# The dt branch of a hybrid block: all 128 partitions, small pieces, a later place in the fill

## The chip, the cores and the metric

The kernel runs on one core of one Trainium2 chip. The metric is device time in microseconds (us) from the first to the last instruction and what lies around them, the median of several runs.

## What is computed

One encoder layer on 512 tokens of width 1024, all in fp32. Cut to what matters here:

```python
h = rms_norm(x, norm1_w)
q, k, v, z, xbc, dt_raw, gate_logits = split_columns(h @ w_in, IN_PROJ_SIZES)
attn = diff_attention(q, k, v, ...) @ w_attn_out          # 8 heads, two softmax maps each
dt_f = softplus(dt_raw[..., :32] + dt_bias_f)              # 32 heads forward, 32 backward
dt_b = softplus(dt_raw[..., 32:] + dt_bias_b)
a_f, a_b = -exp(a_log_f), -exp(a_log_b)
# per chunk of 128 tokens: acs = cumsum(dt * a); exp(acs), exp(acs_last - acs), exp(acs_last) are used
ssd = bi_ssd(...) @ w_ssm_out
x = x + (sigmoid(gate_a) * attn + sigmoid(gate_s) * ssd) @ w_out
x = x + conv_glu(rms_norm(x, norm2_w), ...)
```

The change touches only how the 64 columns of dt_raw are turned into dt and the running sums acs, and when.

## The kernel before

TensorE multiplies in a split form: each fp32 operand is split into hi (rounded, `A.copy` on ScalarE) and lo (`V.tensor_tensor`, the rest, on VectorE), and `mm3` (L201 to L203) makes three matmuls for each 128 rows of the contraction. Weights come through `load_raw` (L133, on SyncE's queue, three buffers `raw`), then as a `RowChunk` (256 columns, two halves of 4 contraction tiles, casts L149 and L150) or a `ColChunk` (two parts of 128 columns, casts L169 and L170), with three buffers each for `whi` and `wlo`.

The first stage is the norm and attention. `attend(fill)` is a planner written out in Python: it keeps a model clock, emits attention's stages (prep: transposes L497; qk: logits L526 and softmax L539 to L546; tr: transposes of the probabilities L552; av: times v L561, with its readers L563 on VectorE and L565 on ScalarE; end: L574 to L580) when their lags are over, and otherwise takes the next step of `fill`. TensorE's instructions run in exactly the order in which this program emits them; the other engines' orders are made by a scheduler. The fill is a chain: the rest of `project(0)`, then `project(1)`, `project(2)`, `project(3)`, then `gate_attn()`. One `project(hp)` makes q, k and v of a pair of heads: three chunks by four token blocks by eight steps of 0.32 us on the model clock, 96 steps, with an evacuation after each block. `v<-mm` (L487) are the four last evacuations of a project; by them project(1) ends near 127 us, project(2) near 181 us and project(3) near 237 us.

PSUM in this stage has eight banks: two under the tag mm (the projections), four under lg (logits), two under t, which everything else shares: tq, ta and av all mean t.

`dt_part` is a generator. It loads 256 columns from C_DT on (only the first 64 are dt), multiplies (`feat_steps`, 8 steps of three matmuls with 512 columns), and works on [64 partitions, 512 tokens]: softplus by a series (L405 to L419: reciprocal in four parts L410, five steps of the series L416), times a (L423), two cumulative sums over 32 partitions each (L426, L427), exp (L428), four stores to DRAM for the later stage (L431). Then eight transposes of 64x128 blocks (L436) into two banks of t, copied out as dtk and acs (L437). Last, selector matmuls (L448) that spread each chunk's last sum, and a tail of two exponentials, a logarithm with its own activation table, and four VectorE operations (L450 to L457). `yield None` ends a piece.

`dt_mixed(fill, dt, lag)` passes the fill's steps on and, each time that they add up to `lag`, takes one piece of dt. Before, the fill given to it is `project(1)`, the lag is 15 us and dt has three pieces: up to the stores; the transposes; the selector and the tail.

Of the kernel before, what the change touches and what calls it, by code (L numbers as in the profile page):

```python
# [8 lines left out]
F32 = mybir.dt.float32  # L9
F32R = mybir.dt.float32r  # L10
# [6 lines left out]
P = 128  # L17
T = 512
D = 1024
NT = T // P  # L20
KD = D // P
# [7 lines left out]
CW = 256  # L29
# [18 lines left out]
def hybrid_block_kernel(ctx: ExitStack, tc, x, w_in, w_attn, w_ssm, w_out, w_up, w_down,  # L48
# [74 lines left out]
    def wtile(tag, shape, dt, bufs):  # L123
        t = wpool.tile([P, 4 * CW], dt, tag=tag, bufs=bufs, name=nm(tag))
        n = shape[0] * shape[1]
        return t[:, :n].rearrange("p (k c) -> p k c", c=shape[1])
# [10 lines left out]
    class RowChunk:  # L137


        def __init__(self, srcs, nk=KD, cw=CW, share=(), between=None):  # L140
            hk = 4 * CW // cw
            self.hk, self.parts = hk, []
            for k0 in range(0, nk, hk):
                n = min(hk, nk - k0)
                raw = load_raw(srcs, k0, n)
                if between and not k0:
                    between()
                hi, lo = wtile("whi", (n, cw), F32R, 3), wtile("wlo", (n, cw), F32R, 3)
                A.copy(hi, raw)  # L149
                (G if k0 in share else V).tensor_tensor(lo, raw, f(hi), SUB)  # L150
                self.parts.append((hi, lo))
# [7 lines left out]
    class ColChunk:  # L159


        def __init__(self, srcs, nk=KD):
            raws = [(k0, min(4, nk - k0), load_raw(srcs, k0, min(4, nk - k0))) for k0 in range(0, nk, 4)]
            self.parts = []
            for j in range(2):
                hi, lo = wtile("whi", (nk, P), F32R, 3), wtile("wlo", (nk, P), F32R, 3)
                for k0, n, raw in raws:
                    src = raw[:, :, j * P:(j + 1) * P]
                    A.copy(hi[:, k0:k0 + n, :], src)  # L169
                    V.tensor_tensor(lo[:, k0:k0 + n, :], src, f(hi[:, k0:k0 + n, :]), SUB)  # L170
                self.parts.append((hi, lo))
# [13 lines left out]
    def wcols(v, c0, n=CW):  # L185
        return v[:, :, c0:c0 + n]
# [99 lines left out]
    def chain(*gens):  # L286
        for g in gens:
            yield from g


    def wide(tag="yb"):
        return mk_yb(tag).rearrange("p a t -> p (a t)")
# [50 lines left out]
    eps = cpool.tile([P, 1], F32, name="eps")  # L343
    elast = cpool.tile([P, NT, 64], F32, name="elast")
    wst = cpool.tile([P, NT, 64], F32, name="wst")
    hd = cpool.tile([64, 2], F32, name="hd")
    na = cpool.tile([64, 1], F32, name="na")

    def table(sp):

# [13 lines left out]
    def parameters(sp):  # L364
        SY.dma_start(pp, pp_d)
        SY.dma_start(rows, rows_d.to_broadcast([P, 4 * 64 + 32]))
        SY.dma_start(hd, hd_d)
        for i in range(2):
            G.tensor_copy(dskip[i * 64:(i + 1) * 64, :], rows[i * 64:(i + 1) * 64, 256 + i::2])
        G.memset(ones, 1.0)  # L370
        G.memset(eps, EPS)
        pr = sp.tile([P, 2, 64], F32, name="pr")
        lv = rows[:, 0:256].rearrange("p (a b d) -> p a b d", a=2, b=2)
        G.tensor_tensor(pr, lv[:, :, 0, :], lv[:, :, 1, :], MUL)
        ls = sp.tile([P, 2], F32, name="ls")
        V.tensor_reduce(ls, pr, AX.X, ADD)
        A.activation(ls, ls, AF.Exp)
        V.tensor_tensor(nlam, ls[:, 1:2], ls[:, 0:1], SUB)
        V.tensor_scalar(nlam, nlam, -LAMBDA_INIT, None, ADD)

        G.tensor_scalar(pp[:, O_CW:O_SN], pp[:, O_CW:O_SN], 0.5, None, MUL)
        for w in range(3):
            c = O_FW + w * 2 * NF
            G.tensor_scalar(pp[:, c:c + NF], pp[:, c:c + NF], 0.5, None, MUL)
        G.tensor_scalar(pp[:, O_FB:O_FB + NF], pp[:, O_FB:O_FB + NF], 0.5, None, MUL)
        G.tensor_scalar(pp[:, O_QN:O_QN + 1], pp[:, O_QN:O_QN + 1], -0.125, None, MUL)
        G.tensor_scalar(pp[:, O_SUB:O_SUB + 1], pp[:, O_SUB:O_SUB + 1], 1.0 - LAMBDA_INIT, None, MUL)
# [8 lines left out]

    def dt_part(ap):

        wdt = ColChunk([wcols(w_in_v, C_DT, CW)])
        ps = yield from feat_steps(wdt, 0, hT)  # L400

        big = [wide("yo") for _ in range(3)]
        halves = [b[:, i:i + T] for b in big for i in (0, T)]
        xx, u, t, t2, p_ = (h[:64] for h in halves[:5])
        V.tensor_scalar(xx, ps[:64, :], hd[:, 0:1], None, ADD)  # L405
        A.activation(u, xx, AF.Abs)
        A.activation(u, u, AF.Exp, scale=-1.0)
        V.tensor_scalar(t, u, 2.0, None, ADD)
        for c in range(NT):
            V.reciprocal(t2[:, c * P:(c + 1) * P], t[:, c * P:(c + 1) * P])  # L410

        V.tensor_tensor(t, u, t2, MUL)
        A.activation(t2, t, AF.Square)
        A.activation(p_, t2, AF.Copy, scale=1.0 / 13.0)
        for c in (11, 9, 7, 5, 3):
            V.scalar_tensor_tensor(p_, p_, 1.0 / c, t2, ADD, MUL)  # L416
        V.scalar_tensor_tensor(p_, p_, 1.0, t, ADD, MUL)
        V.tensor_scalar(xx, xx, 0.0, None, MAX)
        V.scalar_tensor_tensor(p_, p_, 2.0, xx, MUL, ADD)  # L419
        A.activation(na, hd[:, 1:2], AF.Exp)  # L420
        V.tensor_scalar(na, na, -1.0, None, MUL)
        dtf, da, one, acf = p_, u, t, t2
        V.tensor_scalar(da, dtf, na, None, MUL)  # L423
        G.memset(one, 1.0)
        G.memset(one[:, 0:T:P], 0.0)
        V.tensor_tensor_scan(acf[0:32], one[0:32], da[0:32], 0.0, MUL, ADD)  # L426
        V.tensor_tensor_scan(acf[32:64, ::-1], one[32:64], da[32:64, ::-1], 0.0, MUL, ADD)  # L427
        A.activation(xx, acf, AF.Exp)  # L428
        for src, dst in ((acf, acsD), (xx, eacsD)):
            for d in range(2):  # L430
                SY.dma_start(dst.rearrange("g h d l -> d (g h) l")[d], src[d * 32:(d + 1) * 32])  # L431
        yield None
        for src, dst in ((dtf, dtk), (acf, acs)):
            ps = bank("tq")
            for c in range(NT):
                PE.transpose(ps[:, c * 64:(c + 1) * 64], src[:, c * P:(c + 1) * P], ident[:64, :64])  # L436
            V.tensor_copy(dst.rearrange("p c h -> p (c h)"), ps[:, :256])  # L437
        sel = halves[5][:, :2 * P].rearrange("p (d l) -> p d l", d=2)
        G.memset(sel, 1.0)
        for d, row in ((0, P - 1), (1, 0)):  # L440
            G.affine_select(out=sel[:, d, :], in_=sel[:, d, :], pattern=[[0, P]], compare_op=ALU.is_equal,
                            fill=0.0, base=-row, channel_multiplier=1)
        yield None
        ps = bank("tq")
        psv = ps[:, :256].rearrange("p (c h) -> p c h", h=64)
        for d in range(2):
            for c in range(NT):
                PE.matmul(psv[:, c, d * 32:(d + 1) * 32], lhsT=sel[:, d, :], rhs=acs[:, c, d * 32:(d + 1) * 32],  # L448
                          start=True, stop=True)
        A.activation(elast, psv, AF.Exp)  # L450
        V.tensor_tensor(wst, psv, acs, SUB)
        A.activation(wst, wst, AF.Exp)
        V.tensor_tensor(wst, wst, dtk, MUL)

        V.tensor_scalar(dtk, dtk, 1.0e-37, None, MAX)
        A.activation(dtk, dtk, AF.Ln)
        V.tensor_tensor(acs, dtk, acs, SUB)  # L457

    with pool("attn", side="right", reuse_waits="tile") as ap:
# [196 lines left out]
        def dt_mixed(fill, dt, lag):  # L656

            owed = lag
            for step in fill:
                yield step  # L660
                owed += step
                if owed < lag:
                    continue
                owed = 0.0
                for step in dt:
                    if step is None:
                        break
                    yield step
            run(dt)

        def gate_attn():
            for cb in range(4):
                w = ColChunk([wcols(w_in_v, C_GA + cb * CW)])
                gate_a[cb] = mk_yb()
                for j in range(2):
                    ps = yield from feat_steps(w, j, hT)
                    gate_of(gate_a[cb][:, j, :], ps)
                    yield 0.0
# [13 lines left out]
            next(first)  # L692
        parameters(ap)
        with tc.manual_schedule(engines={mybir.EngineType.PE}):
            attend(chain(first, dt_mixed(project(1), dt_part(ap), 15.0), project(2), project(3), gate_attn()))

    phase["stack"].close()
    open_banks("psum2", mm=3, lg=3, t=2)
# [396 lines left out]
```

## Time and profile before

| | |
|---|---|
| three runs | 1244.09, 1251.4, 1351.95 us |
| median | 1251.4 us |
| profiled execution, its own time | 1247.42 us |
| its span from first to last instruction | 1245.6 us |
| mean granted TensorE clock | 0.997 |
| attention stage | from about 7 us to about 297 us of the span |

A row of the trace gives an engine's work by source line and tile (`out<-in`). PE is TensorE, PEld its weight load, DVE VectorE, ACT ScalarE, POOL GpSimd, SPq SyncE's queue. Idle time of TensorE stands in brackets with what ended it. A matmul's own duration overlaps the next one's, so the time that counts is from start to start.

### The profile page before, as it was taken

What the parts mean: (1) busy time and instruction counts of PE and PEld (TensorE: products, weight loads), DVE (VectorE), ACT (ScalarE), POOL (GpSimd) and SP (SyncE); (2) the same over time, 40 slices, a digit from 0 to 9 for tenths busy, and PEclk for the clock granted to TensorE, in tenths of its full rate; (3) what the DMA queues carried; (4) which work ended last, traced back from release to release, by engine and by line L of the source; (5) the groups of instructions that cost most, each with busy time, mean ns of one, the idle gap of its engine ahead of it and who ended that gap; (6) DMA issues with size and microseconds to landing.
All of it is one profiled execution on the core that took longest, in us unless ns stands there. A gap on an engine that the chain in (4) does not pass through costs nothing.

```text
span 1245.6 us, 17543 instructions
## 1 busy us (share of the span) xinstructions
PE 1228.8 (99%) x6552; PEld 1027.3 (82%) x6552; DVE 800.1 (64%) x1389; ACT 639.2 (51%) x1322; POOL 229.3 (18%) x300
## 2 busy tenths in 40 slices
PE   9989999999999999999999999999999999999998
PEld 7989899988887787887878778877888888888887
DVE  5594757563736897777687876595576766663222
ACT  6573858574524667757465663443344444442211
POOL 3221011103003442513433241140000000000000
PEclk9999999999999999999999999999999999999999
DMA  6241222126443544544444343462123333323341
GB/s 215 85 123 44 74 69 79 53 68 169 132 130 114 166 136 135 152 116 139 142 129 136 121 150 102 135 197 92 48 88 102 102 102 102 101 91 97 113 122 37
DMA packets 115016, 140.32 MB, mean 113 GB/s; under 512 B 5321, under 2 KB 96713, under 8 KB 114930
## 3 DMA queue, kind: packets, MB, share of 16 engines
q1 hardware_dynamic: 107762, 114.02, 29.9%
q0 software_dynamic: 7168, 25.17, 6.7%
q8 instruction: 52, 0.85, 0.3%
q14 instruction: 34, 0.28, 0.1%
HBM read 134.68 MB, written 4.49 MB: 112 GB/s over the span
## 4 chain that ended last, share of the span: by engine, by line
PE 88%; DVE 6%; ACT 3%; issue 1%; DMA 1%; POOL 0%; DVEq 0%; SPq 0%; ACTq 0%; POOLq 0%
PE mm L201 23%; PE mm L202 23%; PE mm L203 23%; PE t L561 2%; PE lg L862 2%; PE t L816 2%; PE lg L856 2%; PE lg L201 1%; PE lg L203 1%; PE lg L202 1%; ACT lg L542 1%; DVE lg L539 1%; DMA raw<-in_w_up_dram 1%; PE t L552 1%; PE t L203 1%
## 5 line engine op out<-in xcount | busy, mean ns | idle before, releaser
L170 DVE TENSOR_TENSOR wlo<-raw,whi 128x512 fp32r<-128x512 f32 x268 | 184.3, 717 | 109.0 <-ACT whi L169 105.3
L169 ACT CAST whi<-raw 128x512 fp32r<-128x512 f32 x268 | 155.1, 618 | 169.7 <-PE mm L202 135.4
L201 PE MATMUL mm<-yo,whi 128*128 128x512 f32 (+1 forms) x552 | 214.7, 390 | 0.0
L203 PE MATMUL mm<-yo,wlo 128*128 128x512 f32 (+2 forms) x552 | 213.9, 388 | 0.0
L202 PE MATMUL mm<-yo,whi 128*128 128x512 f32 (+2 forms) x552 | 213.4, 387 | 0.0
L201 PE MATMUL mm<-h,whi 128*128 128x512 f32 x520 | 208.1, 400 | 0.0
L203 PE MATMUL mm<-h,wlo 128*128 128x512 f32 x520 | 206.2, 397 | 0.0
L202 PE MATMUL mm<-h,whi 128*128 128x512 f32 x520 | 205.4, 395 | 0.0
L201 PEld LDWEIGHTS mm<-yo,whi 128*128 128x128 f32 x552 | 103.4, 188 | 22.5 <-issue 1.2
L202 PEld LDWEIGHTS mm<-yo,whi 128*128 128x128 f32 x552 | 103.6, 188 | 21.3 <-issue 0.7
L203 PEld LDWEIGHTS mm<-yo,wlo 128*128 128x128 f32 x552 | 103.6, 188 | 21.2 <-DVE E L795 0.2
L203 PEld LDWEIGHTS mm<-h,wlo 128*128 128x128 f32 x520 | 97.7, 188 | 22.1 <-issue 2.2
L201 PEld LDWEIGHTS mm<-h,whi 128*128 128x128 f32 x520 | 97.8, 188 | 21.4 <-issue 2.4
L202 PEld LDWEIGHTS mm<-h,whi 128*128 128x128 f32 x520 | 97.8, 188 | 20.8 <-issue 2.0
L201 PE MATMUL mm<-whi,h 128*128 128x256 f32 x384 | 114.9, 300 | 0.0
L150 DVE TENSOR_TENSOR wlo<-raw,whi 128x1024 fp32r<-128x1024 f32 x45 | 55.1, 1225 | 89.2 <-ACT whi L149 89.2
L203 PE MATMUL mm<-whi,h 128*128 128x256 f32 x384 | 110.4, 288 | 0.0
L202 PE MATMUL mm<-wlo,h 128*128 128x256 f32 x384 | 110.1, 287 | 0.0
L794 ACT ACTIVATE E<-E,acs 128x128 f32<-128x128 f32 x256 | 79.0, 390 | 29.7 <-POOL E L790 29.7
L149 ACT CAST whi<-raw 128x1024 fp32r<-128x1024 f32 x46 | 48.4, 1051 | 86.5 <-PE lg L203 39.4
L201 PEld LDWEIGHTS mm<-whi,h 128*128 128x128 f32 x384 | 75.0, 196 | 1.4 <-issue 1.1
L202 PEld LDWEIGHTS mm<-wlo,h 128*128 128x128 f32 x384 | 75.2, 196 | 0.0
(236 smaller groups left out, 2139.1 us busy)
## 6 DMA issues: line engine op xcount, KB each, us to landing
raw<-in_w_in_dram SPq DMA_DIRECT2D x74, 512.0 KB, 4.2
raw<-in_w_up_dram SPq DMA_DIRECT2D x44, 512.0 KB, 4.4
E<-acsD POOLq DMA_DIRECT2D x32, 512.0 KB, 5.2
raw<-in_w_down_dram SPq DMA_DIRECT2D x22, 512.0 KB, 3.8
raw<-in_w_in_dram SPq DMA_DIRECT2D x32, 256.0 KB, 4.4
X<-eacsD POOLq DMA_DIRECT2D x32, 256.0 KB, 4.2
raw<-in_w_ssm_dram SPq DMA_DIRECT2D x16, 512.0 KB, 4.6
yb<-in_x_dram SPq DMA_DIRECT2D x8, 512.0 KB, 6.0
```

Of the source, the lines that this page charges most:

```text
L149: A.copy(hi, raw)
L150: (G if k0 in share else V).tensor_tensor(lo, raw, f(hi), SUB)
L169: A.copy(hi[:, k0:k0 + n, :], src)
L170: V.tensor_tensor(lo[:, k0:k0 + n, :], src, f(hi[:, k0:k0 + n, :]), SUB)
L201: PE.matmul(ps, lhsT=lhi, rhs=rhi, start=first, stop=False)
L202: PE.matmul(ps, lhsT=lhi, rhs=rlo, start=False, stop=False)
L203: PE.matmul(ps, lhsT=llo, rhs=rhi, start=False, stop=last)
L561: PE.matmul(po, lhsT=at[:, kb * P:(kb + 1) * P], rhs=vt[:, kb, hh * P:(hh + 1) * P], start=(kb == 0), stop=(kb == NT - 1))
L794: A.activation(v[:, c, :], v[:, c, :], AF.Exp, bias=acs[:, c, s:s + 1])
L816: PE.matmul(ps[:, :n], lhsT=btok[:, c, :], rhs=xw.rearrange("p d q -> p (d q)")[:, :n], start=True, stop=True)
L856: PE.matmul(py[q:q + 64, l], lhsT=xtok[:, c, j * P + q:j * P + q + 64], rhs=W[:, l], start=True, stop=True)
L862: PE.matmul(ps[:, l], lhsT=S[:, i, j * P:(j + 1) * P], rhs=CT[:, l], start=True, stop=True)
```

## The change

dt moves from the fill of project(1) into that of project(2) and project(3), with a lag of 3.0 us and 22 ends of pieces in place of two. Its 64 weight columns are loaded twice, side by side, so that the product stands on all 128 partitions; the first 64 take tokens 0 to 255, the others tokens 256 to 511, and each elementwise operation covers [128, 256] in place of [64, 512]. The reciprocal is two parts of 128 columns in place of four, the sums are four scans over 32 partitions and 256 columns in place of two over 512, the stores eight in place of four, the transposes four of 128x128 in place of eight. Transposes and selector take their banks from mm in place of t. Two `yo` tiles are held in place of three. `ColChunk` gets a width, so that only one part of 128 columns is cast, where before a second one, which nobody used, was cast too.

```diff
@@ ColChunk
-        def __init__(self, srcs, nk=KD):
+        def __init__(self, srcs, nk=KD, cols=CW):
+            n_ = min(P, cols)
-            for j in range(2):
-                hi, lo = wtile("whi", (nk, P), F32R, 3), wtile("wlo", (nk, P), F32R, 3)
+            for j in range(cols // n_):
+                hi, lo = wtile("whi", (nk, n_), F32R, 3), wtile("wlo", (nk, n_), F32R, 3)
...
@@ parameters
-        SY.dma_start(hd, hd_d)
+        for i in range(2):
+            SY.dma_start(hd[i * 64:(i + 1) * 64], hd_d)
@@ dt_part
-        wdt = ColChunk([wcols(w_in_v, C_DT, CW)])
+        wdt = ColChunk([wcols(w_in_v, C_DT, 64)] * 2, cols=P)
         ps = yield from feat_steps(wdt, 0, hT)
-        big = [wide("yo") for _ in range(3)]
-        halves = [b[:, i:i + T] for b in big for i in (0, T)]
-        xx, u, t, t2, p_ = (h[:64] for h in halves[:5])
-        V.tensor_scalar(xx, ps[:64, :], hd[:, 0:1], None, ADD)
+        big = [wide("yo") for _ in range(2)]
+        xx, u, t, t2, p_, sel = (big[i // 4][:, i % 4 * CW:(i % 4 + 1) * CW] for i in range(6))
+        for i in range(2):
+            r = slice(i * 64, (i + 1) * 64)
+            V.tensor_scalar(xx[r], ps[r, i * CW:(i + 1) * CW], hd[r, 0:1], None, ADD)
+        yield None
         A.activation(u, xx, AF.Abs)
         A.activation(u, u, AF.Exp, scale=-1.0)
         V.tensor_scalar(t, u, 2.0, None, ADD)
-        for c in range(NT):
+        for c in range(2):
+            yield None
             V.reciprocal(t2[:, c * P:(c + 1) * P], t[:, c * P:(c + 1) * P])
+        yield None
...
         for c in (11, 9, 7, 5, 3):
+            yield None
             V.scalar_tensor_tensor(p_, p_, 1.0 / c, t2, ADD, MUL)
+        yield None
         V.scalar_tensor_tensor(p_, p_, 1.0, t, ADD, MUL)
         V.tensor_scalar(xx, xx, 0.0, None, MAX)
+        yield None
...
-        V.tensor_tensor_scan(acf[0:32], one[0:32], da[0:32], 0.0, MUL, ADD)
-        V.tensor_tensor_scan(acf[32:64, ::-1], one[32:64], da[32:64, ::-1], 0.0, MUL, ADD)
+        for r in (0, 64):
+            f_, b_ = slice(r, r + 32), slice(r + 32, r + 64)
+            yield None
+            V.tensor_tensor_scan(acf[f_], one[f_], da[f_], 0.0, MUL, ADD)
+            yield None
+            V.tensor_tensor_scan(acf[b_, ::-1], one[b_], da[b_, ::-1], 0.0, MUL, ADD)
         A.activation(xx, acf, AF.Exp)
         for src, dst in ((acf, acsD), (xx, eacsD)):
-            for d in range(2):
-                SY.dma_start(dst.rearrange("g h d l -> d (g h) l")[d], src[d * 32:(d + 1) * 32])
-        yield None
+            for r in range(4):
+                hf, d = divmod(r, 2)
+                SY.dma_start(dst.rearrange("g h d l -> d (g h) l")[d][:, hf * CW:(hf + 1) * CW],
+                             src[r * 32:(r + 1) * 32])
+        for _ in range(4):
+            yield None
         for src, dst in ((dtf, dtk), (acf, acs)):
-            ps = bank("tq")
-            for c in range(NT):
-                PE.transpose(ps[:, c * 64:(c + 1) * 64], src[:, c * P:(c + 1) * P], ident[:64, :64])
-            V.tensor_copy(dst.rearrange("p c h -> p (c h)"), ps[:, :256])
+            ps = bank("mm")
+            for c in range(2):
+                PE.transpose(ps[:, c * P:(c + 1) * P], src[:, c * P:(c + 1) * P], ident)
+            V.tensor_copy(dst.rearrange("p (f c) h -> p c f h", c=2),
+                          ps[:, :CW].rearrange("p (c f h) -> p c f h", f=2, h=64))
...
-        yield None
-        ps = bank("tq")
+        for _ in range(3):
+            yield None
+        ps = bank("mm")
...
@@ the call
-            attend(chain(first, dt_mixed(project(1), dt_part(ap), 15.0), project(2), project(3), gate_attn()))
+            attend(chain(first, project(1), dt_mixed(chain(project(2), project(3)), dt_part(ap), 3.0), gate_attn()))
```

## Rows read from the trace of the kernel before

**Rows 1.** The page, busy time: engine, busy us (share of span), instructions.
```profile
PE 1228.8 (99%) x6552; PEld 1027.3 (82%) x6552; DVE 800.1 (64%) x1389; ACT 639.2 (51%) x1322; POOL 229.3 (18%) x300
```

**Rows 2.** Timeline of TensorE: start, us, instruction, [idle before it <- what ended it].
```profile
77.50 0.66 PE L552 MATMUL t<-ident,lg 128*128 128x128 f32 x4 [1.89 <-ACT osq L565]
...
88.28 0.66 PE L552 MATMUL t<-ident,lg 128*128 128x128 f32 x4 [1.45 <-ACT osq L565]
...
96.75 0.58 PE L561 MATMUL t<-v,at 128*128 128x128 f32 x1 [2.14 <-DVE dtk L437]
...
147.45 0.71 PE L552 MATMUL t<-ident,lg 128*128 128x128 f32 x4 [1.95 <-ACT osq L565]
...
205.24 0.44 PE L552 MATMUL t<-ident,lg 128*128 128x128 f32 x2 [0.58 <-ACT osq L565]
```

**Rows 3.** Stretches: length, busy us (count) of each engine, granted clock, DMA.
```profile
96.73:100.14 3.41, 3.39 (x16) 3.39 (x17) 0.92 (x3) 0.37 (x2) 0.00 (x0) 0.50 0.00 0
147.93:151.34 3.41, 3.41 (x18) 3.41 (x17) 2.31 (x5) 2.08 (x7) 2.00 (x1) 0.50 0.46 133
```

**Rows 4.** Stretches: dt's time before, then each project, then gate_attn's begin.
```profile
60.00:90.00 30.00, 26.66 (x212) 23.80 (x211) 29.97 (x68) 23.44 (x57) 3.56 (x4) 1.00 0.36 104
...
127.00:180.00 53.00, 51.05 (x414) 48.74 (x414) 32.54 (x77) 36.78 (x90) 8.33 (x8) 0.97 0.23 68
180.00:237.00 57.00, 56.42 (x469) 53.44 (x468) 38.26 (x91) 39.74 (x99) 11.41 (x9) 1.00 0.22 64
...
237.00:262.00 25.00, 25.00 (x144) 19.61 (x144) 20.67 (x56) 20.43 (x49) 0.00 (x0) 1.00 0.28 85
```

**Rows 5.** Groups of VectorE, 53 to 127 us, by shape: busy us, mean ns.
```profile
L410 DVE RECIPROCAL yb<-yb 64x128 f32<-64x128 f32 x4 | 3.4, 897 | 0.0
L416 DVE SCALAR_TENSOR_TENSOR yb<-yb,yb 64x512 f32<-64x512 f32 x5 | 3.4, 672 | 0.0
...
L427 DVE TENSOR_TENSOR_SCAN yb<-yb,yb 32x512 f32<-32x512 f32 x1 | 1.2, 1214 | 0.0
...
L423 DVE TENSOR_SCALAR yb<-yb,na 64x512 f32<-64x512 f32 x1 | 0.5, 473 | 0.0
```

**Rows 6.** Groups of VectorE, other stretches: the same and half the width on 128 partitions.
```profile
L546 DVE SCALAR_TENSOR_TENSOR lg<-lg,rs,lg 128x512 f32<-128x512 f32 x32 | 23.6, 747 | 4.7 <-ACT lg L545 4.4
...
L451 DVE TENSOR_TENSOR wst<-t,acs 128x256 f32<-128x256 f32 x1 | 0.4, 420 | 0.0
```

**Rows 7.** The page, costliest groups and DMA issues: casts of a ColChunk, weight loads.
```profile
L170 DVE TENSOR_TENSOR wlo<-raw,whi 128x512 fp32r<-128x512 f32 x268 | 184.3, 717 | 109.0 <-ACT whi L169 105.3
...
raw<-in_w_in_dram SPq DMA_DIRECT2D x74, 512.0 KB, 4.2
```

**Rows 8.** Timelines of TensorE and VectorE, 93 to 97 us: transposes, then the copies.
```profile
93.26 0.81 PE L436 MATMUL t<-ident,yb 64*128 64x64 f32 x8
...
95.29 0.75 DVE L546 SCALAR_TENSOR_TENSOR lg<-lg,rs,lg 128x512 f32<-128x512 f32 x1
...
96.28 0.41 DVE L437 COPY dtk<-t 128x256 f32<-128x256 f32 x1
96.62 0.41 DVE L437 COPY acs<-t 128x256 f32<-128x256 f32 x1
```

**Rows 9.** Timeline of VectorE around the end of project(3).
```profile
234.78 0.29 DVE L563 COPY osb<-t 128x128 f32<-128x128 f32 x1 [1.72 <-PE t L561]
236.15 0.75 DVE L504 SCALAR_TENSOR_TENSOR qkl<-t,pp,qkh 128x512 fp32r<-128x512 f32 x1 [1.07 <-ACT qkh L503]
236.82 0.68 DVE L170 TENSOR_TENSOR wlo<-raw,whi 128x512 fp32r<-128x512 f32 x1
```

**Rows 10.** Timeline of ScalarE: dt's tail with the logarithm's table and the exponential's.
```profile
126.74 0.37 ACT L450 ACTIVATE elast<-t 128x256 f32<-128x256 f32 x1
...
130.95 1.28 ACT L456 ACT_TABLE_LOAD   x1
132.45 0.42 ACT L456 ACTIVATE dtk<-dtk 128x256 f32<-128x256 f32 x1 [0.22 <-DVE dtk L455]
132.89 1.28 ACT L542 ACT_TABLE_LOAD   x1
```

More of the change, by code (lines that the diff above doesn't have):

```diff
@@ L159, in hybrid_block_kernel @@
     class ColChunk:
-        def __init__(self, srcs, nk=KD):
+        def __init__(self, srcs, nk=KD, cols=CW):
+            n_ = min(P, cols)
             raws = [(k0, min(4, nk - k0), load_raw(srcs, k0, min(4, nk - k0))) for k0 in range(0, nk, 4)]
             self.parts = []
-            for j in range(2):
-                hi, lo = wtile("whi", (nk, P), F32R, 3), wtile("wlo", (nk, P), F32R, 3)
+            for j in range(cols // n_):
+                hi, lo = wtile("whi", (nk, n_), F32R, 3), wtile("wlo", (nk, n_), F32R, 3)
                 for k0, n, raw in raws:
-                    src = raw[:, :, j * P:(j + 1) * P]
+                    src = raw[:, :, j * n_:(j + 1) * n_]
                     A.copy(hi[:, k0:k0 + n, :], src)
@@ L345, in hybrid_block_kernel @@
     wst = cpool.tile([P, NT, 64], F32, name="wst")
-    hd = cpool.tile([64, 2], F32, name="hd")
-    na = cpool.tile([64, 1], F32, name="na")
+    hd = cpool.tile([P, 2], F32, name="hd")
+    na = cpool.tile([P, 1], F32, name="na")
     def table(sp):
@@ L424, in dt_part @@
         G.memset(one, 1.0)
-        G.memset(one[:, 0:T:P], 0.0)
-        V.tensor_tensor_scan(acf[0:32], one[0:32], da[0:32], 0.0, MUL, ADD)
-        V.tensor_tensor_scan(acf[32:64, ::-1], one[32:64], da[32:64, ::-1], 0.0, MUL, ADD)
+        G.memset(one[:, 0:CW:P], 0.0)
+        for r in (0, 64):
[4 more added lines that the diff above has]
+            V.tensor_tensor_scan(acf[b_, ::-1], one[b_], da[b_, ::-1], 0.0, MUL, ADD)
         A.activation(xx, acf, AF.Exp)
         for src, dst in ((acf, acsD), (xx, eacsD)):
-            for d in range(2):
-                SY.dma_start(dst.rearrange("g h d l -> d (g h) l")[d], src[d * 32:(d + 1) * 32])
-        yield None
-        for src, dst in ((dtf, dtk), (acf, acs)):
-            ps = bank("tq")
-            for c in range(NT):
-                PE.transpose(ps[:, c * 64:(c + 1) * 64], src[:, c * P:(c + 1) * P], ident[:64, :64])
-            V.tensor_copy(dst.rearrange("p c h -> p (c h)"), ps[:, :256])
-        sel = halves[5][:, :2 * P].rearrange("p (d l) -> p d l", d=2)
+            for r in range(4):
[4 more added lines that the diff above has]
+            yield None
+        for src, dst in ((dtf, dtk), (acf, acs)):
+            ps = bank("mm")
[3 more added lines that the diff above has]
+                          ps[:, :CW].rearrange("p (c f h) -> p c f h", f=2, h=64))
+        sel = sel.rearrange("p (d l) -> p d l", d=2)
         G.memset(sel, 1.0)
```

## The prediction

> **What bounds the kernel now.** I read the page first, for which engine sets the end: TensorE is busy 99% of the span, VectorE 64% [rows 1]. So a change to VectorE's or ScalarE's work can move the end in one way only: through the moments at which TensorE, whose order is fixed by the program, stands before an instruction that waits. Next I went through TensorE's timeline of the attention stage for idle time. It is idle five times for over 0.5 us between 53 and 237 us: 1.89, 1.45, 2.14, 1.95 and 0.58 us [rows 2]. The first three lie in project(1), where dt is, the fourth in project(2), the fifth in project(3). That is 8.01 us in all, out of 1245.6. Then the granted clock: two of these waits, the 2.14 and the 1.95, are followed by a stretch of 3.41 us at 0.50, that is 1.2 GHz in place of 2.4, in which TensorE is busy throughout [rows 3]. At half speed 3.41 us do the work of 1.7, so each such stretch costs 1.7 us more. After the waits of 1.89, 1.45 and 0.58 there is none. All that idle time and clock cost in this stage is therefore 8.01 + 3.4 = 11.4 us, 0.9% of the time. The change can't gain more than that here, plus what it saves of TensorE's own work.
>
> Last, whose fault each wait is. From 60 to 90 us VectorE is busy 29.97 of 30 us, the only stretch where it is full; in project(2) and project(3) together it is busy 70.8 of 110 us [rows 4]. The wait of 2.14 us ends with dt's own copy dtk: the transposes hold both banks of t, and `times_v` needs one. The waits of 1.89, 1.45, 1.95 and 0.58 end with osq, ScalarE's reading of a bank of t, which stands behind softmax work.
>
> **The change, part by part.** The base is the profiled execution, 1247.4 us (span 1245.6 and 1.8 around it). The median of the three runs shown is 1251.4, with 1244.1 below it, so runs differ by several us without any change.
>
> *VectorE's work of dt.* Before, on 64 partitions: four reciprocals 3.4, seven series steps at 0.67 (five L416 and two alike) 4.7, two scans 2.4, the product at L412 0.67, L405 0.74, and three tensor_scalars at 0.41 to 0.47, 1.3: 13.2 us [rows 5]. Nearly all of it lies in 60 to 90 us. A row's duration follows its columns, not its partitions: 64x512 takes 672 ns and 128x512 747 ns, 128x256 420 ns [rows 5, 6]. So after: two reciprocals at 0.90 = 1.8; eight operations of the series and product at 0.42 = 3.4; two additions of 64x256, not shown, taken as 0.42 each = 0.8; three tensor_scalars at half of 0.47, at most 0.28 = 0.8; four scans at half of 1.21 = 2.4. Together 9.2 us, 4 less. The unused second part saves two casts of 0.72 [rows 7]. The scans' half is not shown; if 256 columns cost as much as 512, that is 2.4 us more on VectorE. This work is not on TensorE's path. Its place is what counts.
>
> *Taken out of project(1).* The 2.14 us wait goes for certain, with its 1.7 us of clock: there are no transposes there now, and dt no longer takes banks of t. That is -3.8. The waits of 1.89 and 1.45 come while VectorE is full; without the 13.2 us it would have had about 17 of 30 us. I don't take them as wholly gone, since project(3), with no dt work, still has one of 0.58: -3.34 + 0.58 = -2.8. Bounds: 0 to -3.34.
>
> *Put into project(2) and project(3).* The two have 2 x 96 = 192 steps of 0.32. Owed time starts at the lag, so the first piece comes after step 1 and then one after every ten steps (3.2 is the first sum over 3.0): steps 1, 11, ... 191, twenty pieces in 110 us, one per 5.5 us. The largest holds a reciprocal of 0.90, or a scan, where one run of 3.4 us stood before. 9.2 us on top of 70.8 of 110 us leaves VectorE 27% idle [rows 4], and that idle time is the cover: 0. If the cover fails, a softmax operation behind a piece is late, then its transposes L552 or osq, and the price is that of the same waits in project(1): 0 to +3.3. The 1.95 us in project(2) with its clock I leave where it is: dt's tail, which runs on ScalarE just ahead of it, leaves, but dt's product and casts come. Bounds: -3.65 (gone) to +3.65 (doubled).
>
> *The load and the product.* The same 24 matmuls of 512 columns, at a later place: 0. The load is 256 KB in four DMAs in place of 1 MB in two. A load lands 4.2 us after its issue and is issued a chunk ahead [rows 7]; in project(1) the product waited for nothing [rows 2], and this load stands at the same place of project(2). The four more stores and two more loads on SyncE's queue lie behind scans that end steps 121 to 151, ahead of no load that is short. Cost 0; if it came late, each us of lateness would be a us of TensorE. The Trainium skill's page "DMA: Bandwidth & Descriptors", section Specifications, puts the shortest run at line rate at 512 B; these rows are 256 B. By that rule the load would be slower for its bytes than the rows above; no row here shows a weight load with such runs.
>
> *The end of dt.* This is the new risk. Piece 20, the transposes, comes at step 191, in the midst of the last v block, which holds one bank of mm. So dtf's transposes take the other bank, and acf's must wait until VectorE has copied dtk out. Then one step, and then pieces 21 to 23 follow with nothing between: the selector matmuls wait for the copy of acs. Behind them in TensorE's queue is everything else. Two waits, then, each for a round trip to VectorE. From below: a copy of 0.41 and what it takes to notice, some 0.2 by the idle of ScalarE behind a VectorE result in [rows 10], less 0.36 of the step between: 0.8 for both. From above: twice the wait for the same copy before, 2.14, where the copy stood behind two softmax operations [rows 2, 8], 4.3, and 1.7 for the clock: 6.0. At the end of project(3) VectorE has gaps of 1.7 and 1.07 us and then a block of casts and softmax [rows 9], so I take 1.0 each: +2.0.
>
> *The tail after it.* The exponentials, the two table loads and the logarithm, 0.37 + 0.4 + 1.28 + 0.42 + 1.28 = 3.8 us of ScalarE [rows 10], move to 237 to 262 us, where ScalarE is busy 20.4 of 25 [rows 4]. There the fill is gate_attn's large matmuls, and TensorE has no idle time: 0, at most one wait like the 1.95 with its clock, +3.65. The Trainium skill's page "ScalarE: Activation LUTs", section What ACT_TABLE_LOAD costs, counts 2.66 us for a change of table with its drain. The trace has 1.28 and then at most 0.22 of idle [rows 10], so 1.5; by the page the tail would be 6.4 us and the wait more likely.
>
> *TensorE's own work.* Eight transposes took 0.81 us [rows 8]; four of full size take 0.66 [rows 2]: -0.2.
>
> Sum: -3.8 - 2.8 + 2.0 - 0.2 = -4.8 on 1247.4: 1242.6, said as 1242.5.
>
> **Rivals.**
>
> *Hidden anyway* (0.22). Waits on osq occur in projects without dt's body too, 1.95 and 0.58 [rows 2]; they may belong to the planner's order rather than to dt. Then 1.89 and 1.45 stay, only dtk's 3.8 go, and the end of dt gives back 2.0 to 3.8. Result 1245 to 1248, about 1246.5. Against it: VectorE was full just there.
>
> *The end of dt eats it* (0.15), the case on the other side. The place is step 191 to the selector, the price two waits. If the copies stand behind the block there, a 0.75 and casts of 0.68 [rows 9], four in a row, each wait is some 3 us, and the clock falls after them: 6 + 1.7, and the tail's 3.8 us on ScalarE then cost a wait of 1.95 + 1.7 behind it: 11.4 in all. Against gains of 3.8 + 2.8 + 0.2 = 6.8 that is +4.6: 1252. It decides from 6.8 us on. For it: the copies before came 2.1 us late. Against it: VectorE was full then and is half idle here.
>
> *The load is late* (0.03). If the 256 B runs each took as long as the four times longer runs before, the load would last twice as long as two loads of 4.2, and if none of it were ahead, the product would wait some 8 us: 1250. The page named above speaks for it; that the load is issued ahead speaks against it.
>
> *My forecast* (0.6): 1237 to 1245.
>
> **How the numbers follow.** The forecast's own range is 1237 (the 1.95 us wait and its clock gone too, -3.65, and the end at 0.8) to 1245 (the end at 4.3). Hidden adds up to 1248, the other side up to 1252 and a little over. 1236 to 1252 holds more than eight in ten, with the several us by which runs differ. A measurement tells some 2%, 25 us, from no change. All of the stage's waits together are 11.4 us, so faster by 2% is out of reach of every mechanism here, 0.02; slower by 2% would take several times the worst case of dt's end, 0.02; the same, 0.96.
>
> **What would show it.** Right: in project(1) no wait on dtk, VectorE under 25 of 30 us in 60 to 90, waits on osq there under 0.6, the clock at full from 90 on. Two short waits of TensorE at the end of project(3), for copies at L437's successor, and the Ln table load after them. Wrong: waits on L552 multiplying in project(2), or idle time at dt's end over 4 us with the clock at half behind it, or TensorE waiting for wdt at the begin of project(2).

## The result

The changed kernel is slower. Its median is 1255.6 us (1251.9 to 1257.8, 8 runs), beside 1248.9 us for the kernel before (8 runs, the three shown above among them; the one of 1351.95 us is slow and not in the ratio). The ratio is 1.0053, 95% interval 1.0033 to 1.0073. The forecast was 1242.5 us, and its range, 1236 to 1252, ended below. So size and sign are wrong, though it is still less than 2%. The profiled execution took 1257.0 us, its span 1255.3.

The page's busy times, then TensorE's waits from 40 to 330 us by releaser (us in total, times, longest), of the kernel after. Against [rows 1] TensorE's busy time is the same within 0.4 us, and VectorE's is 2.6 us less.

```profile
PE 1228.4 (98%) x6548; PEld 1025.5 (82%) x6548; DVE 797.5 (64%) x1388; ACT 638.4 (51%) x1320; POOL 226.4 (18%) x300
...
PE mm L202 <- ACT yb L393: 9.7, 1, 9.7
PE t L571 <- ACT osq L584: 5.9, 4, 2.1
PE mm L453 <- DVE dtk L454: 1.7, 1, 1.7
```

The same waits in TensorE's timeline of the kernel after (start, us, instruction, idle before it and what ended it), the answer to [rows 2]:

```profile
106.62 0.50 PE L202 MATMUL mm<-h,whi 128*128 128x512 f32 x1 [0.62 <-ACT whi L170]
...
107.86 0.50 PE L204 MATMUL mm<-h,wlo 128*128 128x512 f32 x1 [0.50 <-DVE wlo L171]
...
132.87 0.66 PE L571 MATMUL t<-ident,lg 128*128 128x128 f32 x4 [1.44 <-ACT osq L584]
...
144.30 1.12 PE L571 MATMUL t<-ident,lg 128*128 128x128 f32 x4 [2.10 <-ACT osq L584]
...
197.00 0.66 PE L571 MATMUL t<-ident,lg 128*128 128x128 f32 x4 [1.35 <-ACT osq L584]
...
230.99 0.44 PE L453 MATMUL mm<-ident,yb 128*128 128x128 f32 x2 [1.68 <-DVE dtk L454]
...
257.75 0.66 PE L571 MATMUL t<-ident,lg 128*128 128x128 f32 x4 [1.06 <-ACT osq L584]
...
308.60 0.80 PE L202 MATMUL mm<-h,whi 128*128 128x512 f32 x1 [9.67 <-ACT yb L393]
```

Its stretches (length, then busy us and count of PE, PEld, DVE, ACT, POOL, then granted clock, DMA share, GB/s): the two that changed most against [rows 4], and the two at half clock, to be read beside [rows 3].

```profile
60.00:90.00 30.00, 30.00 (x249) 27.91 (x248) 22.47 (x59) 24.02 (x61) 5.84 (x6) 1.00 0.21 67
127.00:180.00 53.00, 49.47 (x402) 47.45 (x399) 34.94 (x80) 31.94 (x81) 9.36 (x10) 0.97 0.23 64
...
144.32:147.74 3.42, 3.42 (x16) 3.42 (x17) 2.33 (x8) 2.69 (x7) 1.51 (x2) 0.50 0.55 183
301.34:311.58 10.24, 2.98 (x7) 2.40 (x8) 1.30 (x2) 4.15 (x13) 2.03 (x4) 0.50 0.58 134
```

The account by place, idle time of TensorE and what half clock costs (half of the time that it works at it):

| place | before, us | after, us |
|---|---|---|
| project(1) | 1.89 + 1.45 + 2.14 + 1.7 = 7.2 | 0 |
| project(2) | 1.95 + 1.7 = 3.65 | 0.62 + 0.50 + 1.44 + 2.10 + 1.7 = 6.4 |
| project(3) with dt's end | 0.58 | 1.35 + 1.68 = 3.0 |
| gate_attn | 0 | 1.06 |
| first product of the next stage | 0 | 9.67 + 1.5 = 11.2 |
| sum | 11.4 | 21.7 |

The difference is 10.2 us, and the spans differ by 9.7. The table is of these two executions: the one of the kernel after began 1.5 us faster (the first copy of v of project(0) stands at 41.7 us against 43.2), so some 1 us elsewhere isn't accounted for, and the medians differ by 6.7 us only. Without the last line of the table the change would have gained 0.9 us. So there are two things to explain: a wait of 9.67 us in a stage that the change doesn't touch, and why the rest brought 0.9 us where 4.8 were forecast.

**The wait of 9.67 us.** It is the first matmul of the next stage, and what ends it is the tanh of the last attention gate (L393, L391 before), which reads a bank of mm. ScalarE's timeline of the kernel after, the GpSimd and SyncE issues, and the loads issued from 285 to 310 us (operation, count, KB each, median us to landing):

```profile
298.78 0.62 ACT L170 CAST whi<-raw 128x512 fp32r<-128x512 f32 x1 [3.76 <-issue]
307.43 0.62 ACT L170 CAST whi<-raw 128x512 fp32r<-128x512 f32 x1 [8.03 <-DMA raw<-in_w_attn_dram]
307.96 0.59 ACT L393 ACTIVATE yb<-mm 128x512 f32<-128x512 f32 x1
...
287.63 0.81 POOL L802 DMA_DIRECT2D E<-acsD  x1
...
291.70 0.52 POOL L804 DMA_DIRECT2D X<-eacsD  x1
...
294.40 0.37 SPq L133 DMA_DIRECT2D raw<-in_w_attn_dram  x1
...
E<-acsD POOLq DMA_DIRECT2D x4, 512.0 KB, 9.3
X<-eacsD POOLq DMA_DIRECT2D x4, 256.0 KB, 10.6
raw<-in_w_attn_dram SPq DMA_DIRECT2D x1, 512.0 KB, 13.0
```

The tanh stands behind a cast that waits 8.03 us for a weight load. That load needs 13.0 us, where [rows 7] have 4.2, while 3 MB of broadcast loads for `decay(0)` and `decay(1)`, issued on another engine's queue 3 to 7 us earlier, are for the most part still under way (that they make it late is tested below). The Trainium skill's page "DMA: Bandwidth & Descriptors", section Issuing engines are not separate DMA queues, says that transfers from any issuing engine run on the same 16 DMA engines and interleave; the 13.0 us agree. The Trainium skill's page "PSUM — Partial Sum Buffer", section Engine vs sequencer instructions, calls ScalarE's queue strictly first in, first out; the tanh of 0.59 us behind the cast agrees too.

All of that was so before as well. ScalarE's timeline of the kernel before:

```profile
306.49 0.62 ACT L169 CAST whi<-raw 128x512 fp32r<-128x512 f32 x1 [4.96 <-DMA raw<-in_w_attn_dram]
307.02 0.59 ACT L391 ACTIVATE yb<-mm 128x512 f32<-128x512 f32 x1
```

The tanh ended at 307.6 there, and TensorE didn't wait at all between 285 and 325 us. What differs is the bank. The two banks of mm are taken in turn. dt took one tile of mm before; after, it takes four (product, two transposes, selector). The next stage opens its banks anew, and its first product takes the same bank in both kernels; call it bank 0. Three more tiles turn the order round: if the last gate product lies in bank 1 before, which fits that nothing waited there, it lies in bank 0 after. That this is the cause was put to the test.

### The profile page after: what moved, and what is told of

Same layout as the page of the kernel before. It is cut to its first block, busy times and chain, and to the rows that moved or that the text cites. A ratio compares the mean times of both kernels' runs of the same rounds, so it can differ in the third digit from the quotient of the medians.

```text
span 1255.3 us, 17542 instructions
## 1 busy us (share of the span) xinstructions
PE 1228.4 (98%) x6548; PEld 1025.5 (82%) x6548; DVE 797.5 (64%) x1388; ACT 638.4 (51%) x1320; POOL 226.4 (18%) x300
## 4 chain that ended last, share of the span: by engine, by line
PE 90%; DVE 5%; DMA 2%; ACT 2%; issue 1%; SPq 0%; POOL 0%; DVEq 0%; ACTq 0%
PE mm L202 24%; PE mm L204 24%; PE mm L203 24%; PE lg L881 2%; PE t L835 2%; PE t L580 2%; PE lg L875 2%; PE lg L545 1%; PE lg L204 1%; PE lg L203 1%; PE lg L202 1%; DMA raw<-in_w_attn_dram 1%; PE t L571 1%; DVE lg L558 1%; PE t L204 1%
## 5 line engine op out<-in xcount | busy, mean ns | idle before, releaser
L203 PEld LDWEIGHTS mm<-yo,whi 128*128 128x128 f32 x552 | 103.6, 188 | 21.7 <-issue 0.7
```

Source lines behind the costliest of these rows:

```text
L203: PE.matmul(ps, lhsT=lhi, rhs=rlo, start=False, stop=False)
```

## The experiments

Each was timed in turns with the kernel before; the ratio is to it, with the 95% interval.

### The bank: e1_sel_t, e2_tr_t, e3_before_flip

Three edits that change only the tag from which dt's tiles take their banks. They leave dt three, two and two tiles of mm, so the last gate product lies in bank 1, 0 and 0.

```diff
@@ e1_sel_t, from the kernel after, the selector
-        ps = bank("mm")
+        ps = bank("tq")
@@ e2_tr_t, from the kernel after, the transposes
-            ps = bank("mm")
+            ps = bank("tq")
@@ e3_before_flip, from the kernel before, the selector
-        ps = bank("tq")
+        ps = bank("mm")
```

> The changed kernel with one word changed: the selector matmuls take their bank from t, as before the change, the transposes stay on mm. dt then takes three banks of mm in place of four, so the last gate product of the attention stage falls into bank 1 and the first product of the next stage still into bank 0. Theory A (the wait of 9.67 us at 298 us is a wait for that one bank, whose reader on ScalarE stands behind a cast that waits for a load): the wait is gone, no half clock behind it, time 11 us under the changed kernel's, about 1244, 3 to 6 us under the kernel before by medians. Rival B (the load of w_attn came late by the new timing of the loads, whatever the bank): the wait at the begin of the next stage stays, 8 us or more, time about 1255. By both the other waits stay about as in the changed kernel, 8 to 9 us together.

> The other half alone: the changed kernel with dt's transposes on t, the selector on mm. dt takes two banks of mm, the last gate product falls into bank 0, as in the changed kernel. Theory A: the wait at about 298 us stays, 8 to 10 us, with the clock at half behind it, time 1253 to 1257. Rival C (mm is short of banks because dt's transposes sit there, which delays gate_attn): the wait goes with the transposes, 1244. Rival B: stays as well.

> The kernel before with one word changed: its selector matmuls on mm in place of t, nothing moved. The last gate product then falls into bank 0. Theory A: a wait of 3 to 9 us at about 301 us, for the same reading on ScalarE, in a kernel whose dt is where it was; in the trace of before that reading ends at 307.6 and the next stage's first product starts at about 302, so 5 to 6 us and perhaps half a clock window, time 5 to 9 us above the kernel before. Rivals B and C: no wait there, time as before within 3 us.

Measured: e1_sel_t 1249.4 us, 0.9997 [0.9980, 1.0014]. e2_tr_t 1257.8 us, 1.0078 [1.0049, 1.0107]. e3_before_flip 1260.3 us, 1.0100 [1.0072, 1.0128]. TensorE's waits from 40 to 330 us, of e1_sel_t (all over 0.62 us and one for `bc`), then the longest of e2_tr_t and of e3_before_flip:

```profile
PE t L571 <- ACT osq L584: 5.9, 4, 2.1
PE mm L453 <- DVE dtk L454: 1.7, 1, 1.7
...
PE mm L202 <- DVE bc L743: 0.6, 1, 0.6
```
```profile
PE mm L202 <- ACT yb L393: 9.8, 1, 9.8
```
```profile
PE mm L201 <- ACT yb L391: 9.7, 1, 9.7
```

With an odd number of tiles the wait is absent, with an even number it is there, in the old kernel too, where neither dt's place nor its form was changed. e2_tr_t and e3_before_flip came out slower than expected; e3_before_flip has a second wait of 2.3 us at 125 us (for `v`, the reader of a bank of mm) with its own stretch of half clock. The bank alone explains the whole loss: e1_sel_t can't be told from the kernel before. Its median lies 6.2 us under that of the kernel after, though, where 11 were expected: the profiled executions, which differ by 11.4, are the fastest of its ten and one of the slowest of the other's eight.

### The load behind it: e5_decay_sp, e10_both

```diff
-                G.dma_start(E.rearrange("p d l -> p (d l)"),
+                (SY if p == 0 else G).dma_start(E.rearrange("p d l -> p (d l)"),
...
-                G.dma_start(X[i * 64:(i + 1) * 64].rearrange("p d l -> p (d l)"),
+                (SY if p == 0 else G).dma_start(X[i * 64:(i + 1) * 64].rearrange("p d l -> p (d l)"),
```

e5_decay_sp is this edit of the kernel after, e10_both the same edit of e1_sel_t.

> The changed kernel, banks as they are, but the first eight broadcast loads of the next stage (3 MB for decay(0)) go out on SyncE's queue, three of the four pairs behind the load of w_attn, in place of GpSimd's queue ahead of it. Theory A says that the bank decides whether there is a wait and this load's landing how long it is: landing in 5 to 7 us in place of 13.0, the wait 2 to 4 us in place of 9.67, time 6 to 9 us under the changed kernel's. If the landing does not set the length: the wait stays at 9 to 10 us.

> Edit: e1_sel_t and e5_decay_sp together: the selector on the transposes' banks, and the first pair's decay loads on SyncE's queue. Theory (the first product no longer waits for the gate's bank, and the weight load lands near 297 us instead of 305 to 309 us, so the 0.6 to 3.4 us that the second product of the next stage waited in e1, e4, e7 and e8 go too): no wait over 1 us between 290 and 330 us and no half clock there; 1245 to 1248 us, ratio 0.996 to 0.999. Rival (what waits there depends on the order on ScalarE alone, not on the load): the wait near 314 us stays with 0.6 to 3 us; 1248 to 1251 us.

Measured: e5_decay_sp 1249.2 us, 1.0002 [0.9986, 1.0018]; e10_both 1246.2 us, 0.9986 [0.9973, 1.0000]. TensorE's first product and ScalarE's casts in e5_decay_sp:

```profile
300.06 0.50 PE L202 MATMUL mm<-h,whi 128*128 128x512 f32 x1 [1.54 <-ACT yb L393]
...
298.37 1.14 ACT L170 CAST whi<-raw 128x512 fp32r<-128x512 f32 x2 [3.77 <-issue]
299.41 0.59 ACT L393 ACTIVATE yb<-mm 128x512 f32<-128x512 f32 x1
```

The edit moves the four loads of `decay(0)`, not all eight, as its expectation has it. One of the four still goes out ahead of the weight load, and three behind it; the other four stay on GpSimd's queue ahead of it. The weight load now lands 3.7 us after its issue (293.77 to 297.51). The bank is still the wrong one, so there is a wait, but of 1.54 us. The bank decides whether TensorE waits for the tanh, the load for how long. In e10_both no wait is left there. Its median is 2.4 us below, as the theory had it, but the interval reaches up to 1, so this is a weak result.

### What is late in project(2): e8_no_series

The kernel is e1_sel_t without dt's reciprocals, the VectorE steps of its series and the four scans; dt's numbers and all that follows from them are not computed.

```diff
-            V.reciprocal(t2[:, c * P:(c + 1) * P], t[:, c * P:(c + 1) * P])
...
-            V.scalar_tensor_tensor(p_, p_, 1.0 / c, t2, ADD, MUL)
...
-            V.tensor_tensor_scan(acf[f_], one[f_], da[f_], 0.0, MUL, ADD)
...
+        A.activation(acf, da, AF.Copy)
```

> Edit: e1_sel_t with dt's reciprocals, the products of its logarithm series and its four scans left out (a copy on ScalarE stands for the scans), so dt and everything that comes of it is not computed; pieces, transposes, selector, loads and stores stay. Theory (the bunch of dt's VectorE work between 125 and 138 us makes the osq waits of 1.43 us at 132 and 2.11 us at 143 us): these two become 0.5 us or less each, the wait of 1.68 us for dtk at 229 us stays; 1245 to 1247.5 us. Rival (those waits are of project(2)'s own pattern, as the 1.95 us at 147 us of the kernel before): they stay at 1.4 to 2.2 us, 1248.5 to 1251 us.

Measured: 1248.1 us, 0.9991 [0.9975, 1.0008]. In the trace the waits at 132 and 143 us are gone; what is left of project(2) are the 0.62 and 0.50 us at dt's product and 0.39 us for `sq`. The wait for dtk and those for osq at 192 and 258 us stay. TensorE's waits, then a stretch at half clock (columns as above):

```profile
PE t L561 <- ACT osq L574: 2.7, 3, 1.3
PE mm L202 <- DVE bc L733: 2.5, 1, 2.5
PE mm L443 <- DVE dtk L444: 1.7, 1, 1.7
...
228.44:238.68 10.24, 10.24 (x38) 8.29 (x35) 6.67 (x19) 5.91 (x14) 0.00 (x0) 0.50 0.26 88
```

So the 3.5 us of e1_sel_t in project(2) are dt's VectorE work. The time fell by less than the 2 to 4.5 us expected, and the difference can't be told from 0. The profiled execution shows what took its place. Behind the wait of 1.68 us for dtk, which e1_sel_t has without any loss of clock, come 10.24 us at half clock with TensorE busy throughout, which cost 5.1 us; another 3.41 us at half clock stand at 839 us. And a wait for `bc` in the next stage took 2.5 us in place of 0.6. That one goes with the landing of the same weight load, counted from the issue of the first decay load: 17.6 us later in e1_sel_t, 19.5 here, and 20.4 in e4_all_t below, with 3.4 us of wait. Whether the other executions lost the same isn't shown. So the trace settles what makes the two waits; what their absence is worth in time no run shows.

VectorE's timeline of e1_sel_t shows how the work lies there: the product ahead of dt's series (L419), one of the series steps (L424) and the last scan (L441):

```profile
124.97 0.40 DVE L419 TENSOR_TENSOR yb<-yb 128x256 f32<-128x256 f32 x1
...
132.01 0.42 DVE L424 SCALAR_TENSOR_TENSOR yb<-yb,yb 128x256 f32<-128x256 f32 x1
...
137.46 0.69 DVE L441 TENSOR_TENSOR_SCAN yb<-yb 32x256 f32<-32x256 f32 x1
```

dt's VectorE work begins at 116.8 us, and from 125 to 138 us VectorE runs the whole series and the scans between softmax's operations, with 0.9 us of idle time in the stretch. The pieces were to come one per 5.5 us, up to 228 us. They do so on TensorE alone, where the order is the program's; VectorE's order is made by a scheduler, and there the steps stand close together.

### Place and form apart: e6_place, e7_p1_fine, e4_all_t

```diff
@@ e6_place, from the kernel before: old dt, new place
-            attend(chain(first, dt_mixed(project(1), dt_part(ap), 15.0), project(2), project(3), gate_attn()))
+            attend(chain(first, project(1), dt_mixed(chain(project(2), project(3)), dt_part(ap), 15.0), gate_attn()))
@@ e7_p1_fine, from e4_all_t: new dt, old place
-            attend(chain(first, project(1), dt_mixed(chain(project(2), project(3)), dt_part(ap), 3.0), gate_attn()))
+            attend(chain(first, dt_mixed(project(1), dt_part(ap), 1.5), project(2), project(3), gate_attn()))
@@ e4_all_t, from the kernel after, twice: transposes and selector
-            ps = bank("mm")
+            ps = bank("tq")
```

> Edit: the kernel before with dt moved alone: still 64 partitions, three pieces with a lag of 15, but filled into the projections of the third and fourth pair instead of those of the second. Theory (VectorE runs dt as a bunch wherever it stands, and the attention products around it wait for osq): the waits of 1.89, 1.45 and 2.14 us of the kernel before at 77 to 97 us go, and waits of together 4 to 9 us come up in 105 to 160 us, half clock in one or two places; 1245 to 1251 us. Rival (the third and fourth projections have room, as the forecast had it): waits of at most 2 us more there, 1239 to 1243 us.

> Edit: the changed kernel's dt (128 partitions, 22 pieces, transposes and selector on the transposes' banks) put back to the old place, the fill of the second pair's projections, with a lag of 1.5. Theory (the pieces order TensorE only; VectorE's order bunches them): waits for osq in 60 to 100 us stay, 3 to 6 us together instead of 5.5 us, the waits at 133 and 143 us shrink to the 1.95 us of the kernel before; 1244 to 1250 us. Rival (the work per instruction is what cost in the old place; half the VectorE work removes it): waits of under 1.5 us in 60 to 100 us and no half clock there, 1240 to 1243 us.

> Edit: transposes and selector product of the changed kernel both back on the transposes' banks (in e1 only the selector went back), so that dt takes one tile of the products' banks, as before the change. Theory (the last gate product in bank 1 is all that matters for the 9.67 us wait): no wait above 1 us between 290 and 315 us, no half clock there, 1247 to 1251 us, equal to e1_sel_t; the wait of 1.68 us at 229 us becomes under 0.5 us since the transposes no longer hold up the next product. Rival (the wait at dt's end is made by VectorE being late with the copies, whatever bank they go to): the 1.68 us wait stays with 1.3 to 2.1 us.

Measured: e6_place 1248.3 us, 1.0002 [0.9985, 1.0019]; e7_p1_fine 1251.3 us, 1.0016 [0.9993, 1.0039]; e4_all_t 1249.0 us, 1.0002 [0.9982, 1.0021]. None can be told from the kernel before. TensorE's waits of e6_place (two lines) and of e7_p1_fine:

```profile
PE t L552 <- ACT osq L565: 5.1, 3, 2.0
PE t L436 <- ACT at L554: 1.2, 1, 1.2
```
```profile
PE t L571 <- ACT osq L584: 4.7, 4, 3.1
PE mm L202 <- ACT E L813: 3.0, 1, 3.0
PE t L453 <- DVE dtk L454: 1.4, 1, 1.4
```

The place alone moves the waits along: the old dt in project(2) gives 1.79, 1.40 and 1.96 us at 132, 143 and 198 us, nearly where the new dt has them. The form alone in the old place gives one of 3.1 us at 85 us, and at dt's end, at 119 to 121 us, waits of 1.4 and 0.7 us with 6.83 us at half clock. In e4_all_t the wait for dtk at 229 us is gone, as expected, but that for osq at 254 us grew from 1.06 to 1.84 us, and the 3.4 us for `bc` at 314 us, with 3.41 us at half clock behind them, were not expected.

### A place that is free: e9_late, e11_late_sp, e12_late_few

If VectorE runs dt in one go wherever its product stands, the place should be where attention is ending. In e1_sel_t VectorE is busy 10.2 of 25 us from 262 to 287 us. In e9_late dt's VectorE work came somewhat earlier, from 257 to 271 us; from 256 to 272 us VectorE is busy 9.3 of 16 us in e1_sel_t and 14.2 in e9_late.

```diff
@@ e9_late, from e1_sel_t
-        def dt_mixed(fill, dt, lag):
-            owed = lag
+        def dt_mixed(fill, dt, lag, start=0.0):
+            owed = lag - start
...
-            attend(chain(first, project(1), dt_mixed(chain(project(2), project(3)), dt_part(ap), 3.0), gate_attn()))
+            attend(chain(first, project(1), project(2), project(3), dt_mixed(gate_attn(), dt_part(ap), 0.6, 16.0)))
@@ e12_late_few, from e9_late; 20 of the 22 ends of pieces in dt_part are taken out too
-            attend(chain(first, project(1), project(2), project(3), dt_mixed(gate_attn(), dt_part(ap), 0.6, 16.0)))
+            attend(chain(first, project(1), project(2), project(3), dt_mixed(gate_attn(), dt_part(ap), 6.0, 16.0)))
```

e11_late_sp is e9_late with the edit of e5_decay_sp.

> Edit: e1_sel_t with dt moved once more, out of the projections into the attention gate's products, started 16 us of products into them (about 262 us), one piece per step. Theory (e8_no_series: dt's VectorE work costs 3.5 us of osq waits where it lies beside the attention's densest part; behind the fourth pair's last attention VectorE is nearly idle): the waits of 0.62, 0.50, 1.43, 2.11 and 1.68 us of e1_sel_t go, the two at 132 and 143 us become under 0.5 us each, at dt's end and in its stage up to 2 us come up; 1243 to 1247 us, ratio to the kernel before 0.995 to 0.998. Rival (dt so late holds up what needs it: decay's loads are issued behind its stores, ScalarE's tanh and exponentials behind its pieces): a wait of 4 us or more between 285 and 340 us, with half clock; 1248 to 1256 us.

> Edit: e9_late with the first pair's decay loads on SyncE's queue as in e10_both. Theory (what is left of the waits at the stage's end in e9_late, 0.37 us, is small, and the queue's order decided only through that wait): 1239 to 1242 us, no difference from e9_late that can be measured. Rival (the load's landing still costs something there): 1236 to 1239 us.

> Edit: e9_late with dt handed out in three pieces (product and all of its VectorE work; transposes; selector) with a lag of 6 instead of 22 pieces with a lag of 0.6. Theory (the yields between VectorE's steps place only what TensorE issues; VectorE's own order comes from the scheduler): VectorE still runs dt as a bunch, the same waits within 1 us together; 1239 to 1242.5 us. Rival (the small pieces keep dt out of the attention's way): osq waits of 1.5 to 4 us more between 255 and 285 us; 1242.5 to 1246 us.

Measured: e9_late 1240.1 us (1238.3 to 1244.1), 0.9939 [0.9919, 0.9959]. e11_late_sp 1239.7 us, 0.9920 [0.9901, 0.9938]. e12_late_few 1247.2 us, 0.9980 [0.9966, 0.9994]. The waits of e9_late:

```profile
PE t L571 <- ACT osq L584: 1.0, 2, 0.7
PE mm L202 <- ACT yb L393: 0.9, 1, 0.9
PE mm L203 <- DVE wlo L150: 0.8, 1, 0.8
PE mm L453 <- DVE dtk L454: 0.5, 1, 0.5
PE mm L202 <- DVE bc L743: 0.4, 1, 0.4
```

That is 3.6 us in all and no half clock in the stage, against 11.4 us before: 7.8 us less, and the medians differ by 8.4. Both kernels, e9_late and e11_late_sp, beat the one before and the changed one; between the two nothing can be told. e9_late came out below the 1243 to 1247 us expected. The theory had counted 6.3 us to go and up to 2 us to come back; it left out the waits of 1.33 and 1.06 us at 195 and 256 us, of which 0.3 us is left. One wait for osq, of 0.73 us at 131 us, is over the 0.5 expected, though dt is no longer there.

e12_late_few met neither theory nor rival. The waits for osq stay at 1.0 us, as the theory had it, but others come. TensorE's timeline of e12_late_few, then VectorE's:

```profile
272.50 0.41 PE L444 MATMUL mm<-ident,yb 128*128 128x128 f32 x2 [0.74 <-DVE yb L423]
276.18 0.69 PE L444 MATMUL mm<-ident,yb 128*128 128x128 f32 x2 [3.27 <-DVE dtk L445]
...
272.85 0.68 DVE L432 TENSOR_TENSOR_SCAN yb<-yb 32x256 f32<-32x256 f32 x1
...
275.70 0.42 DVE L445 COPY dtk<-mm 128x256 f32<-128x256 f32 x1
```

And in e9_late:

```profile
270.47 0.69 DVE L441 TENSOR_TENSOR_SCAN yb<-yb 32x256 f32<-32x256 f32 x1
...
275.92 0.44 PE L453 MATMUL mm<-ident,yb 128*128 128x128 f32 x2 [0.52 <-DVE dtk L454]
```

VectorE's order of dt is the same in both, one bunch. With three pieces the transposes come while it is still at the series, and TensorE waits 4.0 us behind the scans, with 3.41 us at half clock after it. With 22 pieces they come 4 us after the last scan. So this is what small pieces do: they don't spread VectorE's work, they are the distance at which TensorE follows it. Of the 12.1 us between the two profiled spans, 4.7 are from before dt: the wait of 0.73 us that both have for osq ends at 136.0 us in one and at 131.3 in the other. All of these 4.7 us arise ahead of 27 us: up to 23.2 us most matmuls of 128x256 take 0.41 us in e12_late_few, as at half clock in the kernel after, and in e9_late 0.28 us from 16.3 us on. The edit doesn't explain that; why the full clock came later is open. e12_late_few's profiled execution is the slowest of its twelve runs and e9_late's the fastest of its eight; the medians differ by 7.1 us.

The old form at the late place wasn't tried: attention's results for three pairs hold six of the eight `yo` tiles there, and the old dt needs three more. So what the form may have brought is that place, with its two tiles; no run shows it.

## Why the prediction was wrong

*What bounds the kernel.* Right: TensorE's waits and its clock were the only currency, and the 10.2 us of waits and clock fit the 9.7 us between the spans. But I looked for waits between 53 and 262 us only and bounded the change by 11.4 us of that stage. The loss lies at 308 us.

*Taken out of project(1).* Right. No wait is left there, VectorE is at 22.5 of 30 us, the clock is full: the 6.6 us counted (3.8 and 2.8) came as 7.2.

*Put into project(2) and project(3), at 0.* Wrong, and this term took back most of the gain. The step that failed is "steps 1, 11, ... 191, one per 5.5 us", which was taken for VectorE's order. VectorE's work was sized well (9.7 us in the trace against 9.2, the scans 0.68 in place of 0.6), but it came within 21 us, its series and scans within the last 13, and the 27% idle of the whole stretch were no cover for it. project(2) went from 3.65 to 6.4 us and project(3) without dt's end from 0.58 to 1.35. Together that is +3.5, a little over the upper bound of +3.3; I had taken 0. Of the waits in project(2), e8_no_series shows 3.5 us, those at 132 and 143 us, to be dt's VectorE work. I had also left the 1.95 us of project(2) where it was, as its own; without dt's VectorE work 0 (e8_no_series) to 0.73 us (e9_late) of waits for osq are left there. The 1.35 us in project(3) stay in e8_no_series, and what makes them is open. The 0.62 and 0.50 us at dt's product are no late load: the casts of its weights come late in ScalarE's order, while the load, in e1_sel_t's trace, landed at 95.6 us, 11 us before them; the rival of the late load is out. Of the forecast's own signs of being wrong one came, the waits for osq in project(2), two in place of one.

*The end of dt.* The size was right, 1.68 us against 2.0 for two waits (only one came). The step that failed here is another: it missed what else the tags mean. I saw that transposes and selector change from t to mm, and asked only who holds a bank of mm at that moment. That three more tiles turn round all later turns of the two banks, up to the next stage, was not in the sum, so it stood there at nothing, and it is the 11.2 us, the largest error of the forecast. No rival had it either. e1_sel_t and e3_before_flip show it by one tag each.

*The tail.* Between the bounds: 1.06 us at 257 us against 0 to 3.65, with no half clock. (0.37 + 0.4 + 0.42 and two times 2.66 us are 6.5 us, not the 6.4 that stand there.) The rival by which dt's end eats the gain came out 3.6 us from its time, 1252, but by luck, not by its mechanism: the wait at dt's end has 1.68 of the 7.7 us it needed.

*Hidden anyway.* Without the bank, this is nearly the case that came: the waits moved instead of going (e1_sel_t, e6_place, both at 1.000), and 1246.5 us lies within 3 us of them. Its reason was another one, though: the waits are dt's own, at the old place as at the new.

## What to carry to other kernels

Where PSUM banks are handed out in turn, a change in how many tiles a stage takes changes which bank each later product meets; count the tiles modulo the banks up to the next point where they begin anew, and look at what reads the last ones. In a program that orders one engine by hand, pieces between two of its instructions say nothing of the other engines' order: look in the trace where their work lies, and place the whole of it where that engine has room (here 257 to 271 us, worth 8 us). A wait that is hidden, as the tanh behind a load that took 9.6 to 13 us, is a price waiting for the first change that uncovers it.

## What the hardware showed besides

The clock fell during the long wait itself, at 301.3 us, and stayed at 0.50 for 10.24 us in all three kernels that have it. Around 2 us of idle time it is not settled by the length: 2.10 us at 144.30 in the kernel after was followed by 3.4 us at 0.50, 2.11 us at the same place in e1_sel_t by none; 1.68 us for dtk was followed by 10.24 us at 0.50 in e8_no_series and by none in e1_sel_t. The same 512 KB load took 3.7 us with three of the eight decay loads issued behind it, and with all of them ahead on another engine's queue 13.0 us, or 9.6 in the kernel before. A scan of 32x256 takes 0.68 us against 1.21 for 32x512, so a little over half.
